# The 31-tap convolution of two recurrences: VectorE's taps behind the triangular inverse, and four taps moved from GpSimd

## The chip, the cores and the metric

The kernel runs on one core of a Trainium2 chip. The metric is the device time of one launch in microseconds (us). Engines are called PE (TensorE; PEld is its weight load), DVE (VectorE), ACT (ScalarE), POOL (GpSimd) and SP (SyncE, which issues most DMAs).

## What is computed

The reference runs two streams of 256 tokens and 1024 features, `ctx` and `x`, through two layers. Each layer normalises and modulates, projects with `w_in`, sends one half of the projection through a gated depthwise convolution of 31 taps and the other half through a linear recurrence in both directions, projects with `wo`, and ends with a SwiGLU block. The convolution, on which all of this turns:

```python
def conformer_conv(u, conv_w, conv_b, cnorm_g, cnorm_b):
    val, gate = jnp.split(u, 2, axis=-1)
    z = val * jax.nn.sigmoid(gate)
    z = dwconv(z, conv_w) + conv_b          # CONV_K = 31, 512 features
    z = group_norm(z, CONV_GROUPS, cnorm_g, cnorm_b, LN_EPS)
    return jax.nn.silu(z)
```

The recurrence is `s = s * w + sa * b + v * k` over the tokens, per head of 64, forward and backward. The kernel computes it in chunks, which needs the inverse of many small unit-triangular matrices.

## The kernel before

Activations lie feature-major, 128 features by 256 tokens; the convolution has four such blocks f0 to f3. `first()` runs the phases in this order: `wide(0, ctx)`, the first recurrence; the projections of `x`; the recurrence of layer 0 `x` beside the feed-forward of `ctx` with the middle convolution spread among them; the recurrence of layer 1 `ctx` without outputs; output and feed-forward of `x`; `wide(1, x)`, the last recurrence. A second function with no convolution of this kind runs the rest.

`wide` builds the recurrence with a filler beside it (the projection of the convolution's input, whose gated result is stored at L670 as `x0`, tile name `x` or `x0_67`, and matmuls of the modulation weights, `pb<-raw,csil`). In program order, after the whole recurrence, stands `conv`. The recurrence has these steps on the way:

- `inverse`: 31 steps, each a DVE multiply (L961) and a DVE subtract (L963), every one needing the one before.
- two DVE transposes of the result (L966, L968), small matmuls, and the building of Q: GpSimd clears its two tiles (L986), DVE and ACT copy (L982, L994) and negate (L1008, L1010).
- beside these, the products that prepare the recurrence (DVE at L1028 and L1064).
- `chain`: two groups of heads with four steps each. A step runs PE, DVE L1093, PE, ACT L1101 and DVE L1102, PE, DVE L1110 and L1111 (L1113 in a first step), and ends in the output (ACT L1130 or DVE L1132).

`conv` splits the 30 side taps of each block: the innermost to DVE as a fused multiply-add on the tile `T1c` (L725, started by L718 with the middle tap), the next to ACT (a scaled copy, L729) and the outermost to GpSimd (a scaled copy into a tile `tap`, L731). GpSimd adds every `tap`, ACT's too, into the result (L732). `tap` has two buffers, so ACT's taps and GpSimd's wait for those adds. L736 on DVE adds `T1c` to GpSimd's sum and closes a block; it needs GpSimd's last add of that block. A pair in `NPOOL` (first recurrence) or `NPOOLE` (last) gives GpSimd's and ACT's taps. With (14, 3) DVE has 13, with (12, 4) it has 14. `NPOOLC` belongs to the middle convolution (tile `z`), all of it on GpSimd.

Each engine works off its queue in order. The order is fixed ahead of time by a scheduler, which fills each engine's idle time of a simulated timeline with ready work and prefers what stands earlier in the program. So it is the schedule, and not the source, that decides that DVE's taps stand between the steps of the inverse.

Of the kernel before, what the change touches and what calls it, by code (L numbers as in the profile page):

```python
# [12 lines left out]
ALU = mybir.AluOpType  # L13
# [21 lines left out]

NLAST = 2, 4

NPOOL, NPOOLE, NPOOLC = (14, 3), (12, 4), (30, 0)
NTAP = 2

QB, QE, QC, EVERY = (2, 3, 4, 5), (2, 3, 4, 5), (1,), 2
# [217 lines left out]
class Prog:  # L259
# [427 lines left out]
    def mixed_in(self, conv, y, perm=False):  # L687

        mix = self.mixtiles()
        for f in range(NF):  # L690
            src = (conv if f < 4 else y)[:, f % 4, :]
            if perm:
                t = self.T1([P, T])
                a, b = self.unperm(t, src, True)
                self.nc.gpsimd.tensor_copy(a, b)
                src = t
            self.split(src, *mix[f])
        return mix

    def conv(self, l, z, acc, npool, hold=False):  # L700


        nc = self.nc
        o = COLS[f"convw{l}"][0]
        taps = sorted((j for j in range(31) if j != 15), key=lambda j: abs(j - 15))
        nv, na = 30 - npool[0] - npool[1], npool[1]
        parts = [("v", taps[:nv]), ("a", taps[nv : nv + na]), ("p", taps[nv + na :])]

        order = []
        for k, js in parts:  # L710
            order += [((i + 0.5) / len(js), k, j) for i, j in enumerate(js)]
        order.sort()
        zc = [acc[:, f, :] for f in range(4)]
        for f in range(4):
            w = lambda j: self.cols[:, o + 4 * j + f : o + 4 * j + f + 1]
            av = self.T1([P, T]) if nv else None
            if nv:
                nc.vector.tensor_scalar(av, z[:, f, :], w(15), None, ALU.mult)  # L718
                nc.gpsimd.memset(zc[f], 0.0)
            else:  # L720
                nc.gpsimd.tensor_scalar(zc[f], z[:, f, :], w(15), None, ALU.mult)
            for i, (_, k, j) in enumerate(order):
                d, s = slice(max(0, 15 - j), min(T, T + 15 - j)), slice(max(0, j - 15), min(T, T + j - 15))
                if k == "v":
                    nc.vector.scalar_tensor_tensor(av[:, d], z[:, f, s], w(j), av[:, d], ALU.mult, ALU.add)  # L725
                else:
                    t = self.t(self.pool, [P, T], "tap", bufs=NTAP)
                    if k == "a":
                        nc.scalar.mul(t[:, d], z[:, f, s], w(j))  # L729
                    else:  # L730
                        nc.gpsimd.tensor_scalar(t[:, d], z[:, f, s], w(j), None, ALU.mult)  # L731
                    nc.gpsimd.tensor_add(zc[f][:, d], zc[f][:, d], t[:, d])  # L732
                if i % 5 == 4:
                    yield
            if nv:
                nc.vector.scalar_tensor_tensor(zc[f], av, self.col(f"convb{l}", f), zc[f], ALU.add, ALU.add)  # L736
            else:
                nc.gpsimd.tensor_scalar(zc[f], zc[f], self.col(f"convb{l}", f), None, ALU.add)
            yield
        while hold and not self.go:  # L740
            yield
        self.group_norm(zc, f"cng{l}", f"cnb{l}", LN_EPS, AF.Silu)
# [200 lines left out]
    def inverse(self, Ld, Lo):  # L943

        nc = self.nc
        fl = lambda t: t.rearrange("p d a c x -> p (d a c) x")
        Ld, Lo = fl(Ld), fl(Lo)  # L950
        tj = self.S([P, 32, 32])
        nc.vector.transpose(tj.rearrange("p r c -> p c r"), Ld.rearrange("p j c -> p c j"))
        X = self.S([P, 32, 32])
        nc.gpsimd.memset(X, 0.0)
        xf = X.rearrange("p r c -> p (r c)")
        nc.gpsimd.memset(xf[:, 0:1024:33], 1.0)
        for k in range(31):
            m = 31 - k
            tmp = self.T1([P, 256])
            tv = tmp[:, 0 : m * (k + 1)].rearrange("p (a b) -> p a b", b=k + 1)  # L960
            nc.vector.tensor_mul(tv, tj[:, k + 1 : 32, k : k + 1].broadcast_to([P, m, k + 1]),  # L961
                                 X[:, k : k + 1, 0 : k + 1].broadcast_to([P, m, k + 1]))
            nc.vector.tensor_sub(X[:, k + 1 : 32, 0 : k + 1], X[:, k + 1 : 32, 0 : k + 1], tv)  # L963
        yield
        qt = self.S([P, 32, 32])
        nc.vector.transpose(qt, X)  # L966
        qc = self.S([P, 32, 32])
        nc.vector.transpose(qc, X.rearrange("p r c -> p c r"))  # L968

        zss = []  # L970
        for d in range(2):
            pz = self.ps((P, 16, 32))
            zs = Lo[:, 16 * d : 16 * d + 16, :]
            for j in range(16):
                J = 16 * d + j
                for h in range(2):
                    r = slice(64 * h + 32, 64 * h + 64)
                    w = slice(64 * h, 64 * h + 32)
                    self.mm(pz[w, j, :], Lo[r, J, :], qt[r, :, J], tile_position=(64 * h + 32, 64 * h))
            for h in range(2):  # L980
                w = slice(64 * h, 64 * h + 32)
                (nc.scalar.copy if h else nc.vector.tensor_copy)(zs[w], pz[w])  # L982
            zss.append(zs)
        Q = [self.S([P, 16, CH]) for _ in range(2)]
        for d in range(2):
            nc.gpsimd.memset(Q[d], 0.0)  # L986
            js = slice(16 * d, 16 * d + 16)
            src, zs = (qt, qc)[d], zss[d]
            po = self.ps((P, 16, 32))
            for q in range(4):  # L990
                s = slice(32 * q, 32 * q + 32)
                o = (q % 2) * 32
                dst, v = Q[d][s, :, o : o + 32], src[s][:, :, js].rearrange("p c j -> p j c")
                (nc.vector.tensor_copy if q % 2 else nc.scalar.copy)(dst, v)  # L994
            for j in range(16):
                J = 16 * d + j
                for h in range(2):
                    w = slice(64 * h, 64 * h + 32)
                    r = slice(64 * h + 32, 64 * h + 64)
                    if d == 0:  # L1000
                        self.mm(po[w, j, :], qc[w, :, J], zs[w, j, :], tile_position=(64 * h, 64 * h))
                    else:
                        self.mm(po[r, j, :], zs[w, j, :], qc[w, :, J], tile_position=(64 * h, 64 * h + 32))
            for h in range(2):
                w = slice(64 * h + 32 * d, 64 * h + 32 * d + 32)
                dst = Q[d][w, :, 32 * (1 - d) : 32 * (1 - d) + 32]
                if h:
                    nc.scalar.mul(dst, po[w], -1.0)  # L1008
                else:
                    nc.vector.tensor_scalar(dst, po[w], -1.0, None, ALU.mult)  # L1010
        self.Q = Q
# [626 lines left out]
```

## Time and profile before

| | us |
|---|---|
| median of 3 runs | 2772.72 (2772.6 to 2775.5) |
| the profiled execution | 2776.2 |
| its span | 2774.1 |
| PE busy | 2628.3 (95%) |
| DVE busy | 1713.4 (62%) |
| ACT busy | 1327.6 (48%) |
| POOL busy | 667.0 (24%) |

The span is what lies between the first and the last recorded instruction, 2.1 us less than the time of the execution. A busy PE is not PE at its peak, since matmul ends are modelled and its clock is granted at 1.2 or 2.4 GHz (0.50 or 1.00 of full speed). GpSimd's 667 us lie almost wholly in the stretches from 133 to 575 us (the first and the middle convolution) and from 1165 to 1280 us (the last).

### The profile page before, as it was taken

How to read it: one execution, taken by the hardware profiler on the slowest of the kernel's cores; microseconds unless marked ns; L12 is line 12 of the kernel's file. 1: busy time of each engine (PE TensorE's matmuls, PEld its weight loads, DVE VectorE, ACT ScalarE, POOL GpSimd, SP SyncE). 2: the span in 40 equal slices, each digit the busy share in tenths (PEclk: the TensorE clock that was granted, in tenths of full speed). 3: DMA queues.
4: the chain of work that ended last, by engine and by line, in shares of the span. 5: the costliest groups of instructions: out<-in, count | busy, mean ns of one | idle time of the engine just before them, and what ended most of it. 6: DMA issues, size and time to landing. Idle time of an engine off the chain costs nothing.

```text
span 2774.1 us, 53770 instructions
## 1 busy us (share of the span) xinstructions
PE 2628.3 (95%) x22398; PEld 2288.3 (82%) x22398; DVE 1713.4 (62%) x2703; ACT 1327.6 (48%) x2015; POOL 667.0 (24%) x669
## 2 busy tenths in 40 slices
PE   7889988999889998899899899999999999999998
PEld 4866867888678897866799899889899898889897
DVE  3885778655577555984555655666655655755655
ACT  5533654434564346433544544654544544644543
POOL 0287999920130001384200000010000000100000
PEclk9989989999999999979899999999999999999999
DMA  7244424434323354234355555524555554525653
GB/s 251 102 153 167 153 86 167 139 129 145 137 77 115 130 181 148 100 138 153 124 188 183 198 184 188 188 86 157 183 186 186 183 186 172 170 85 183 205 185 119
DMA packets 118767, 430.70 MB, mean 155 GB/s; under 512 B 13174, under 2 KB 13686, under 8 KB 118524
## 3 DMA queue, kind: packets, MB, share of 16 engines
q1 hardware_dynamic: 118524, 427.28, 44.7%
q8 instruction: 175, 2.87, 0.4%
q14 instruction: 68, 0.56, 0.1%
HBM read 425.13 MB, written 2.10 MB: 154 GB/s over the span
## 4 chain that ended last, share of the span: by engine, by line
PE 76%; DVE 10%; POOL 5%; ACT 5%; issue 2%; DMA 2%; SPq 0%; ACTq 0%; POOLq 0%; DVEq 0%
PE pb L333 32%; PE acc L333 24%; PE ps L333 19%; POOL tap L731 3%; DVE wl L342 2%; POOL z L732 1%; DVE T1c L725 1%; DMA raw<-in_ada 1%; DVE S L963 1%; DVE T L961 1%; POOL x L732 1%; ACT wh L341 1%; PE acc L438 0%; DMA raw<-in_wr 0%; ACT L384 0%
## 5 line engine op out<-in xcount | busy, mean ns | idle before, releaser
L342 DVE TENSOR_TENSOR wl<-raw,wh 128x1024 fp32r<-128x1024 f32 (+1 forms) x654 | 814.5, 1249 | 621.6 <-ACT wh L341 390.9
L341 ACT CAST wh<-raw 128x1024 fp32r<-128x1024 f32 (+1 forms) x654 | 681.8, 1046 | 892.7 <-PE pb L333 349.8
L333 PE MATMUL pb<-xf,wh 128*128 128x256 f32 (+1 forms) x2560 | 488.1, 289 | 15.6 <-DVE T1b L588 5.2
L333 PE MATMUL pb<-S,wh 128*128 128x256 f32 x2560 | 490.9, 289 | 4.3 <-DVE S L462 1.8
L333 PEld LDWEIGHTS pb<-xf,wh 128*128 128x128 f32 (+1 forms) x2560 | 411.3, 195 | 29.7 <-DVE T1b L588 8.8
L333 PEld LDWEIGHTS pb<-S,wh 128*128 128x128 f32 x2560 | 407.7, 192 | 21.5 <-issue 11.7
L333 PE MATMUL ps<-S,wh 128*128 128x256 f32 x2048 | 390.6, 288 | 0.5 <-ACT S L460 0.4
L333 PE MATMUL pb<-xf,wl 128*128 128x256 f32 (+1 forms) x1280 | 372.8, 292 | 8.9 <-DVE wl L342 8.9
L365 POOL TENSOR_TENSOR wl<-raw,wh 128x1024 fp32r<-128x1024 f32 x22 | 52.1, 2379 | 1340.7 <-ACT wh L364 824.2
L333 PE MATMUL pb<-S,wl 128*128 128x256 f32 x1280 | 367.4, 287 | 2.1 <-DVE wl L342 2.1
L333 PEld LDWEIGHTS ps<-S,wh 128*128 128x128 f32 x2048 | 327.0, 192 | 9.4 <-issue 3.7
L333 PE MATMUL ps<-S,wl 128*128 128x256 f32 x1024 | 293.8, 287 | 0.6 <-DVE wl L342 0.6
L333 PEld LDWEIGHTS pb<-xf,wl 128*128 128x128 f32 (+1 forms) x1280 | 249.3, 195 | 16.9 <-DVE wl L342 11.7
L333 PEld LDWEIGHTS pb<-S,wl 128*128 128x128 f32 x1280 | 245.3, 192 | 7.0 <-issue 3.2
L333 PE MATMUL acc<-wh,T 128*128 128x512 f32 x704 | 206.3, 393 | 0.0
L333 PEld LDWEIGHTS ps<-S,wl 128*128 128x128 f32 x1024 | 196.7, 192 | 3.0 <-issue 1.5
L333 PE MATMUL acc<-wh,T1b 128*128 128x512 f32 x528 | 158.6, 399 | 3.5 <-ACT T1b L341 3.5
L731 POOL TENSOR_SCALAR tap<-z,cols 128x255 f32<-128x255 f32 (+14 forms) x120 | 154.4, 1295 | 0.0
L333 PEld LDWEIGHTS acc<-wh,T 128*128 128x128 f32 x704 | 127.0, 189 | 23.6
L731 POOL TENSOR_SCALAR tap<-x,cols 128x246 f32<-128x246 f32 (+6 forms) x104 | 112.9, 1093 | 46.1 <-DVE x L670 46.0
L333 PEld LDWEIGHTS acc<-wh,T1b 128*128 128x128 f32 x528 | 94.9, 190 | 22.3 <-ACT T1b L341 4.4
L333 PE MATMUL acc<-wl,T 128*128 128x512 f32 x352 | 113.3, 395 | 0.0
(445 smaller groups left out, 3956.7 us busy)
## 6 DMA issues: line engine op xcount, KB each, us to landing
raw<-in_fu SPq DMA_DIRECT2D x132, 512.0 KB, 3.2
raw<-in_ada SPq DMA_DIRECT2D x96, 512.0 KB, 4.2
raw<-in_pu SPq DMA_DIRECT2D x88, 512.0 KB, 4.3
raw<-in_qu SPq DMA_DIRECT2D x88, 512.0 KB, 4.2
raw<-in_fd SPq DMA_DIRECT2D x66, 512.0 KB, 3.2
raw<-in_wr SPq DMA_DIRECT2D x51, 512.0 KB, 3.9
raw<-in_pd SPq DMA_DIRECT2D x44, 512.0 KB, 4.3
raw<-in_qd SPq DMA_DIRECT2D x44, 512.0 KB, 4.3
```

What stands on the lines that cost most here:

```text
L333: return self.nc.tensor.matmul(out, lhsT, rhs, start=start, stop=stop, **kw)
L341: self.nc.scalar.copy(hi, src)
L342: self.nc.vector.tensor_sub(lo, src, hi.bitcast(F32))
L365: self.nc.gpsimd.tensor_sub(lo, r, hi.bitcast(F32))
L725: nc.vector.scalar_tensor_tensor(av[:, d], z[:, f, s], w(j), av[:, d], ALU.mult, ALU.add)
L731: nc.gpsimd.tensor_scalar(t[:, d], z[:, f, s], w(j), None, ALU.mult)
L732: nc.gpsimd.tensor_add(zc[f][:, d], zc[f][:, d], t[:, d])
L961: nc.vector.tensor_mul(tv, tj[:, k + 1 : 32, k : k + 1].broadcast_to([P, m, k + 1]), X[:, k : k + 1, 0 : k + 1].broadcast_to([P, m, k + 1]))
L963: nc.vector.tensor_sub(X[:, k + 1 : 32, 0 : k + 1], X[:, k + 1 : 32, 0 : k + 1], tv)
```

## The change

Two things change. The pairs of taps become (10, 3) and (9, 3): in the first recurrence DVE takes four taps more of each block and GpSimd four fewer; in the last DVE takes four more, GpSimd three fewer and ACT one fewer. And the first DVE instruction of each block is not issued before the last subtract of the inverse.

```diff
-NPOOL, NPOOLE, NPOOLC = (14, 3), (12, 4), (30, 0)
+NPOOL, NPOOLE, NPOOLC = (10, 3), (9, 3), (30, 0)
...
             if nv:
-                nc.vector.tensor_scalar(av, z[:, f, :], w(15), None, ALU.mult)
+                with self.tc.issue_after(self.inverted.ins):
+                    nc.vector.tensor_scalar(av, z[:, f, :], w(15), None, ALU.mult)
                 nc.gpsimd.memset(zc[f], 0.0)
...
-            nc.vector.tensor_sub(X[:, k + 1 : 32, 0 : k + 1], X[:, k + 1 : 32, 0 : k + 1], tv)
+            self.inverted = nc.vector.tensor_sub(X[:, k + 1 : 32, 0 : k + 1], X[:, k + 1 : 32, 0 : k + 1], tv)
```

Behind L718 all line numbers grow by one. The change moves instructions in the queues, so here is what stands there at three places.

DVE's queue in the first recurrence, near the end of the inverse, before:

```order
L725 SCALAR_TENSOR_TENSOR T1c_3011<-x_67,cols,T1c_3011 128x252
L961 TENSOR_TENSOR T_205_1273<-S_1187,S_1189 128x112
L725 SCALAR_TENSOR_TENSOR T1c_3011<-x_67,cols,T1c_3011 128x252
L963 TENSOR_TENSOR S_1189<-S_1189,T_205_1273 128x4x28
L725 SCALAR_TENSOR_TENSOR T1c_3011<-x_67,cols,T1c_3011 128x251
L961 TENSOR_TENSOR T_206_1276<-S_1187,S_1189 128x87
L725 SCALAR_TENSOR_TENSOR T1c_3011<-x_67,cols,T1c_3011 128x251
L963 TENSOR_TENSOR S_1189<-S_1189,T_206_1276 128x3x29
```

The same place with the change:

```order
L962 TENSOR_TENSOR T_207_1279<-S_1187,S_1189 128x60
L964 TENSOR_TENSOR S_1189<-S_1189,T_207_1279 128x2x30
L962 TENSOR_TENSOR T_208_1282<-S_1187,S_1189 128x31
L964 TENSOR_TENSOR S_1189<-S_1189,T_208_1282 128x31
L719 TENSOR_SCALAR T1c_2875<-x_67,cols 128x256
L719 TENSOR_SCALAR T1c_2935<-x_67,cols 128x256
L726 SCALAR_TENSOR_TENSOR T1c_2875<-x_67,cols,T1c_2875 128x255
L726 SCALAR_TENSOR_TENSOR T1c_2935<-x_67,cols,T1c_2935 128x255
```

The taps leave the inverse and start right behind its last subtract, two blocks side by side; the transpose L967 (before L966) comes 16 rows later.

DVE's queue in the first recurrence, around the step that closes the fourth block (L736, then L737, on `x1_68`), before, from the last L1102 of the chain on:

```order
L1102 TENSOR_SCALAR xf_261_1607<-acc10_424_2673 64x2x128
L342 TENSOR_TENSOR wl_578_3279<-raw_576_3276,wh_577_3278 128x1024
L1110 TENSOR_TENSOR st_426_2693<-acc11_425_2684,st_412_2585 128x256
L1111 TENSOR_TENSOR st_426_2693<-st_426_2693,pc_149_884 128x256
...
L342 TENSOR_TENSOR wl_586_3343<-raw_584_3340,wh_585_3342 128x1024
L736 SCALAR_TENSOR_TENSOR x1_68<-T1c_531_3079,cols_69,x1_68 128x256
L936 TENSOR_TENSOR T1_467_2835<-acc00_466_2831,S_62_299 128x256
```

With the change:

```order
L1094 TENSOR_TENSOR T1_359_2299<-acc00_358_2290,Sb_243_1503 128x256
L1065 TENSOR_TENSOR T2_274_1677<-acc11_272_1667,const_70 64x256
L1065 TENSOR_TENSOR T2_274_1677<-acc10_273_1668,const_70 64x256
L1103 TENSOR_SCALAR xf_242_1502<-acc00_361_2302 64x2x2x64
L1065 TENSOR_TENSOR T2_277_1690<-acc11_275_1680,const_70 64x256
L503 TENSOR_TENSOR mod0_82<-pb_378_2388,cols_69 128x8
L508 SCALAR_TENSOR_TENSOR mod0_82<-mod0_82,cols_69 128x16
L737 SCALAR_TENSOR_TENSOR x1_68<-T1c_519_3055,cols_69,x1_68 128x256
L1065 TENSOR_TENSOR T2_277_1690<-acc10_276_1681,const_70 64x256
L1103 TENSOR_SCALAR xf_261_1607<-acc10_333_2183 64x2x2x64
```

Before, the closing step stands behind the whole chain. Now it stands behind two of the chain's eight L1103 steps and ahead of the other six.

DVE's queue in the last recurrence, around the same closing step, before:

```order
L1111 TENSOR_TENSOR st_2388_14152<-st_2388_14152,pc_2170_12672 128x256
L1102 TENSOR_SCALAR xf_2282_13395<-acc10_2414_14262 64x2x2x64
L1093 TENSOR_TENSOR T1_2426_14338<-acc00_2425_14329,Sb_2264_13291 128x256
L736 SCALAR_TENSOR_TENSOR x1_68<-T1c_2527_14821,cols_69,x1_68 128x256
L503 TENSOR_TENSOR mod1_83<-pb_2410_14244,cols_69 128x8
L1110 TENSOR_TENSOR st_2416_14282<-acc11_2415_14273,st_2360_14023 128x256
```

With the change:

```order
L1065 TENSOR_TENSOR T2_2282_13446<-acc10_2281_13437,const_70 64x256
L737 SCALAR_TENSOR_TENSOR x1_68<-T1c_2499_14765,cols_69,x1_68 128x256
L1094 TENSOR_TENSOR T1_2340_13968<-acc10_2339_13959,Sb_2267_13364 128x256
L1094 TENSOR_TENSOR T1_2368_14097<-acc00_2367_14088,Sb_2248_13259 128x256
L1103 TENSOR_SCALAR xf_2266_13363<-acc10_2342_13971 64x2x2x64
L1103 TENSOR_SCALAR xf_2247_13258<-acc00_2370_14100 64x2x2x64
```

Before, four of the eight L1102 steps stand ahead of it; now one, and seven follow.

## Rows read from the trace of the kernel before

**Rows 1.** The chain of waits of the page: its share by engine.
```profile
PE 76%; DVE 10%; POOL 5%; ACT 5%; issue 2%; DMA 2%; SPq 0%; ACTq 0%; POOLq 0%; DVEq 0%
```

**Rows 2.** Busy time by stretch: us, engines with instructions, PE clock, DMA share, GB/s.
```profile
1170.00:1180.00 10.00, 8.05 (x112) 7.23 (x112) 10.00 (x18) 2.11 (x4) 9.68 (x11) 1.00 0.30 107
380.00:440.00 60.00, 44.71 (x606) 36.82 (x605) 49.53 (x69) 33.69 (x65) 59.63 (x59) 0.86 0.23 80
```

**Rows 3.** Busy time by stretch of DVE alone, first and last recurrence's inverse.
```profile
113.00:187.50 74.50, 68.14 (x155) 0.89 0.44 149
1149.00:1220.00 71.00, 69.65 (x155) 0.95 0.45 157
```

**Rows 4.** The same stretches, T1c's instructions alone: PE, PEld, DVE, ACT, then clock.
```profile
113.00:187.50 74.50, 0.00 (x0) 0.00 (x0) 26.10 (x43) 0.00 (x0) 0.89 0.44 149
1149.00:1220.00 71.00, 0.00 (x0) 0.00 (x0) 26.52 (x46) 0.00 (x0) 0.95 0.45 157
```

**Rows 5.** DVE's timeline, first recurrence: start us, duration us, line, operation, [idle before].
```profile
187.18 0.17 DVE L963 TENSOR_TENSOR S<-S,T 128x31 f32<-128x31 f32 x1
187.38 1.25 DVE L966 STREAM_TRANSPOSE S<-S 128x1024 f32<-128x1024 f32 x1
188.55 1.92 DVE L968 STREAM_TRANSPOSE S<-S 128x1024 f32<-128x1024 f32 x1
190.39 0.38 DVE L1064 TENSOR_TENSOR T<-acc,const 64x256 f32<-64x256 f32 x1
190.80 3.47 DVE L994 COPY S<-S 32x512 f32<-32x512 f32 x4
...
224.65 0.43 DVE L1102 TENSOR_SCALAR xf<-acc 64x256 f32<-64x256 f32 x1 [2.04 <-PE acc L333]
...
264.59 0.43 DVE L1102 TENSOR_SCALAR xf<-acc 64x256 f32<-64x256 f32 x1 [0.58 <-PE acc L333]
...
277.49 0.69 DVE L736 SCALAR_TENSOR_TENSOR x<-T1c,cols,x 128x256 f32<-128x256 f32 x1
```

**Rows 6.** One line's instructions: count, shortest, median and longest ns, first and last start.
```profile
L725 DVE SCALAR_TENSOR_TENSOR T1c<-x,cols,T1c x108: 459/568/1021, 134.6 to 1243.9; 128x255 f32<-128x255 f32 x16, 128x254 f32<-128x254 f32 x16, 128x253 f32<-128x253 f32 x16, 128x252 f32<-128x252 f32 x16
L732 POOL TENSOR_TENSOR x<-x,tap x132: 691/716/1618, 134.9 to 1279.2; 128x247 f32<-128x247 f32 x16, 128x246 f32<-128x246 f32 x16, 128x245 f32<-128x245 f32 x16, 128x244 f32<-128x244 f32 x16
L731 POOL TENSOR_SCALAR tap<-x,cols x104: 888/1038/2128, 133.0 to 1277.5; 128x246 f32<-128x246 f32 x16, 128x245 f32<-128x245 f32 x16, 128x244 f32<-128x244 f32 x16, 128x243 f32<-128x243 f32 x16
```

**Rows 7.** GpSimd's timeline, first recurrence: start us, duration us, line, [idle before].
```profile
133.03 1.89 POOL L731 TENSOR_SCALAR tap<-x,cols 128x247 f32<-128x247 f32 x2 [24.08 <-DVE x L670]
...
276.46 2.81 POOL L731 TENSOR_SCALAR tap<-z,cols 128x255 f32<-128x255 f32 x2
```

**Rows 8.** What GpSimd's adds (L732) of both convolutions waited for: us, times.
```profile
  ACT tap L729: 28.5, 8
```

**Rows 9.** DVE's timeline, last recurrence, same columns as rows 5.
```profile
1219.48 0.39 DVE L963 TENSOR_TENSOR S<-S,T 128x31 f32<-128x31 f32 x1
...
1279.91 0.48 DVE L736 SCALAR_TENSOR_TENSOR x<-T1c,cols,x 128x256 f32<-128x256 f32 x1 [5.61 <-POOL x L732]
...
1295.83 0.43 DVE L1102 TENSOR_SCALAR xf<-acc 64x256 f32<-64x256 f32 x1
```

**Rows 10.** ACT's timeline, last recurrence, same columns: a tap, then chain steps.
```profile
1274.29 0.50 ACT L729 ACTIVATE tap<-x,cols 128x247 f32<-128x247 f32 x1 [4.93 <-POOL x L732]
...
1288.45 0.38 ACT L1101 ACTIVATE xf<-acc 64x256 f32<-64x256 f32 x1
1292.00 0.38 ACT L1101 ACTIVATE xf<-acc 64x256 f32<-64x256 f32 x1 [3.17 <-PE acc L333]
```

**Rows 11.** GpSimd's timeline, last recurrence: the first tap.
```profile
1165.26 1.00 POOL L731 TENSOR_SCALAR tap<-x,cols 128x246 f32<-128x246 f32 x1 [21.90 <-DVE x L670]
```

**Rows 12.** Chain of waits, 380 to 440 us (start, us, what), and one wait there.
```profile
395.68 5.09 POOL S L847 x2
...
DVE T L961 <- POOL S L956: 4.9, 1, 4.9
```

## The prediction

> **What bounds the kernel now.** I read the chain of waits first: PE holds 76% of it, DVE 10%, POOL 5% [rows 1]. Outside the two long recurrences the weights' matmuls fill PE, and there a change to DVE or GpSimd is worth nothing. So the question is only what PE loses in three stretches: the first recurrence (113 to 270 us), the last (1149 to 1300 us), and 380 to 440 us, where GpSimd works at the middle convolution. I read busy time by stretch next. In 1170 to 1180 us PE is busy 8.05 of 10 us while DVE shows 10.00 and POOL 9.68 [rows 2]: the inverse and the taps share a full DVE, and the splits of weights that feed PE stand in the same queue. In 380 to 440 us PE misses 15.3 of 60 us, POOL is busy 59.63 [rows 2], and POOL stands on the chain of waits there: two L847 take 5.09 us, and an inverse waits 4.9 us for a GpSimd memset [rows 12]. Last come the timelines of DVE, ACT and GpSimd, for what ends when.
>
> **Term 1: the inverse loses its taps.** From its start to its last subtract DVE is busy 68.14 of 74.5 us in the first recurrence and 69.65 of 71 us in the last [rows 3]. Of this the taps are 26.10 us (43 instructions, 0.607 each) and 26.52 us (46, 0.577 each) [rows 4]. All of them go behind the inverse. Its last subtract ends at 187.4 and 1219.9 us now [rows 5, 9]; without the taps it would end at 161.3 and 1193.4 us. I add about 2 us of waits for PE that the taps filled until now: 163 and 1195 us.
>
> **Term 2: what DVE must do behind it.** The taps come back, and more of them. In the first recurrence a block has 17 + L718 + L736, which is 19 for each of four blocks and 76 in all (60 before); in the last 18 + 2, so 80 (64 before). At 0.607 and 0.577 us that is 46.1 and 46.2 us. By the order with the change these stand, with some 40 others, ahead of L737 of the fourth block, and ahead of most of the chain. The others are 15 or 16 of L1064 at about 0.4 us (6.3 us), the two transposes (3.2), four L994 (3.5) [rows 5], and some 20 smaller ones, for which I estimate 6.6 us from instructions of this size: 19.6 us. So DVE reaches the closing step at 163 + 46.1 + 19.6 = 228.7 us in the first recurrence, and at 1195 + 46.2 + 19.6 = 1260.8 us in the last. In the first recurrence two chain steps are done by then, in the last one.
>
> **Term 3: GpSimd.** A tap takes 1.04 us and an add 0.72 (medians) [rows 6]. The first recurrence loses 16 of each, 28.2 us; the last 12 taps and 16 adds, 24.0 us (four of these adds were for ACT's taps, which cost ACT 0.50 us each [rows 10] and are otherwise free). GpSimd's first convolution runs from 133.0 to 276.5 us [rows 7]. It would end at 248 if its waits for ACT's taps stay, and at 220 if all 28.5 us of these [rows 8] go. ACT's taps now stand in ACT's queue behind copies that wait for the transposes, so some stay: I take 238 us. The last runs from 1165.3 to 1279.9 us [rows 9, 11] and would end near 1256, ahead of DVE.
>
> **Term 4: a new wait.** Before, L736 of the fourth block stood behind the chain's eight L1102 and ran at 277.5 us, after the last of them at 264.6 [rows 5]; nothing stood behind it that mattered. Now L737 needs GpSimd's last add with six chain steps queued behind it. In the first recurrence DVE is there at 228.7 and GpSimd at 238: DVE stands for 9 us, and the chain with it, PE's outputs of the recurrence next. In the last recurrence GpSimd comes first and the wait costs nothing; it costs what GpSimd is late beyond 1260.8 if ACT's taps come late.
>
> **Term 5: the chain's end.** A step without taps between takes 3.6 us (L1101 at 1288.45 and 1292.00) [rows 10]. Before, ACT's taps, each waiting for a GpSimd add (4.93 us at 1274.29 [rows 10]), stood between the steps; with the change the last of ACT's taps comes before the second step. First: 238 + 6 x 3.6 = 259.6 against 264.6 us [rows 5], a gain of 5.0. PE has filler in either case, and the same amount of it. Last: 1260.8 + 7 x 3.6 = 1286.0 against 1295.8 [rows 9], a gain of 9.8.
>
> **Term 6: the middle convolution.** GpSimd turns to it about 38 us earlier (238 against 276.5), and the same number of its instructions, 111, stands between its start and the first L365 in both orders. So at 380 us GpSimd should no longer be late. It can give back at most the 15.3 us that PE misses there [rows 2] and at least nothing, since L847 and the memset still run there. I take 7 us, near the middle and close to the 5.09 and 4.9 us of rows 12 together with little else.
>
> **Sum.** 5.0 + 9.8 + 7 = 21.8 us off the profiled execution's 2776.2 us: 2754.4. That execution lies 3.5 us above the median 2772.72, so the forecast is 2751 us. Ends: the first term runs from a loss of 5 (GpSimd at 248) to a gain of 14 (DVE decides at 228.7); the last from a gain of 19 (taps at the shortest 0.459 us [rows 6]) to a loss, below; the middle from 0 to 15.
>
> **A rule against it.** A tap takes 0.459 us at its shortest, 0.568 in the median and 1.021 at its longest [rows 6], and the mean beside a GpSimd that was busy 9.68 of 10 us was 0.577. The Trainium skill says in "SBUF — State Buffer", section "SBUF: two separate sides", that VectorE with two SBUF inputs and GpSimd take a shared port pair as an exclusive lock, and the loser blocks for the other's whole instruction. By that every tap that meets a GpSimd instruction would pay for it in full, which is the first rival below with a price beyond it. The trace agrees only in part: both engines show nearly 10 of 10 us busy at once, and the taps are stretched by a quarter, not doubled; but recorded times can hold waiting.
>
> **Rivals.** (a) Taps that stand in a row next to GpSimd are stretched more than those between the inverse's steps. At 0.92 us, near the longest, the first recurrence has DVE at the closing step at 163 + 69.9 + 19.6 = 252.5 and the chain's end at 274.1, 9.5 us late; the last has 1195 + 73.6 + 19.6 + 25.2 = 1313.4, 17.6 late. With nothing from the middle the kernel takes 2772.7 + 27 = 2800 us. It decides from 0.79 us a tap in the first recurrence and 0.70 in the last. Against it: the means of rows 4 were taken beside the same GpSimd instructions. (b) The closing step's wait and PE's fill eat the first recurrence: GpSimd at 248, no gain in the middle because the recurrence there is later reached by the same in-order queue, and only the last recurrence's 9.8 less 5 stays: 2768 us, within 0.2%. (c) All three stretches pay in full, 14 + 19 + 15: 2725 us. For it speaks that PE also lost clock there; against it that DVE's queue is full in each case. (d) The change doesn't do what it says: taps still between the inverse's steps. The order excludes it.
>
> **How the numbers follow.** A run of this kernel can tell about 0.2% from no change, 5.5 us: faster is below 2767.2, slower above 2778.3. Forecast (gain of 8 to 36 us): 0.64. (c): 0.07. (b), from 2764 to 2778: 0.16, a fifth of it faster. (a): 0.13, nearly all slower. So faster 0.74, same 0.13, slower 0.13. The range 2733 to 2777 holds the forecast's own spread and (b), and leaves out most of (a) and (c).
>
> **What would show it.** Right: the last subtract near 163 and 1195 us; the fourth L737 near 238 (after a wait for GpSimd) and 1261; the last L1103 near 260 and 1286; T1c at 0.55 to 0.62 us behind the inverse; GpSimd's middle convolution from 238 us and PE missing about 8 us in 380 to 440. Wrong: a T1c mean above 0.7, the closing step waiting beyond 248, an inverse that still ends after 175 or 1205 because PE and not DVE paced it, or PE missing as much as before around 380 to 440.

## The result: slower by 1.2%

The change takes 2806.4 us (median of four runs) against 2772.7 us before, a ratio of 1.0119 (95% interval 1.0103 to 1.0135). Forecast were 2751 us. I split each profiled execution at four events of DVE's timeline: the start of the first inverse (first L961), the last L1102 of the first chain, the start of the last inverse, the last L1102 of the last chain (starts, each time). A stage's time is that of one profiled execution of its kernel.

| us | before | change | difference |
|---|---|---|---|
| first inverse's start to first chain's end | 151.2 | 163.8 | +12.6 |
| first chain's end to last inverse's start | 885.1 | 882.2 | -2.9 |
| last inverse's start to last chain's end | 146.1 | 167.0 | +20.9 |
| the whole span | 2774.1 | 2803.7 | +29.6 |

The loss lies in the two recurrences. DVE's timeline of the change (start us, duration us, line, operation, [idle before]; all lines behind L718 are one higher than before), first and last recurrence, answers to [rows 5, 9]:

```profile
111.92 0.19 DVE L962 TENSOR_TENSOR T<-S,S 128x31 f32<-128x31 f32 x1
...
161.18 0.57 DVE L964 TENSOR_TENSOR S<-S,T 128x31 f32<-128x31 f32 x1
...
193.34 0.68 DVE L1011 TENSOR_SCALAR S<-ps 32x512 f32<-32x512 f32 x1
214.14 0.43 DVE L1103 TENSOR_SCALAR xf<-acc 64x256 f32<-64x256 f32 x1
...
230.59 0.43 DVE L1103 TENSOR_SCALAR xf<-acc 64x256 f32<-64x256 f32 x1
...
235.77 0.48 DVE L737 SCALAR_TENSOR_TENSOR x<-T1c,cols,x 128x256 f32<-128x256 f32 x1 [3.12 <-POOL x L733]
...
275.74 0.43 DVE L1103 TENSOR_SCALAR xf<-acc 64x256 f32<-64x256 f32 x1
```

```profile
1157.93 0.20 DVE L962 TENSOR_TENSOR T<-S,S 128x31 f32<-128x31 f32 x1
...
1201.62 0.60 DVE L964 TENSOR_TENSOR S<-S,T 128x31 f32<-128x31 f32 x1
...
1254.81 0.43 DVE L1103 TENSOR_SCALAR xf<-acc 64x256 f32<-64x256 f32 x1
...
1274.39 0.47 DVE L737 SCALAR_TENSOR_TENSOR x<-T1c,cols,x 128x256 f32<-128x256 f32 x1
...
1324.94 0.43 DVE L1103 TENSOR_SCALAR xf<-acc 64x256 f32<-64x256 f32 x1
```

Before, each inverse begins and the first of the chain's L1102 runs at:

```profile
113.44 0.19 DVE L961 TENSOR_TENSOR T<-S,S 128x31 f32<-128x31 f32 x1
...
218.06 0.43 DVE L1102 TENSOR_SCALAR xf<-acc 64x256 f32<-64x256 f32 x1
```

```profile
1149.68 0.22 DVE L961 TENSOR_TENSOR T<-S,S 128x31 f32<-128x31 f32 x1
...
1255.92 0.43 DVE L1102 TENSOR_SCALAR xf<-acc 64x256 f32<-64x256 f32 x1 [4.49 <-PE acc L333]
```

The inverse ends about where it was forecast, 24 and 26 us sooner after its start than before (at 161.8 us, and 44.3 us after its start in the last recurrence). The closing step L737 comes at 235.8 and 1274.4 us. But the chain, which had its eight L1102 in 46.5 us in the first and 39.9 in the last recurrence before (first L1102 to last), now takes 61.6 and 70.1 us. It begins sooner and ends later.

**What stands behind the taps.** The products of L1064 (now L1065) prepare the chain's two groups and stand in DVE's queue among the taps. Their rows before and after, first and then last recurrence (count: shortest/median/longest ns, first to last start):

```profile
L1064 DVE TENSOR_TENSOR T<-acc,const x16: 376/416/418, 174.4 to 217.6; 64x256 f32<-64x256 f32 x16
L1064 DVE TENSOR_TENSOR T<-acc,const x16: 402/408/418, 1206.0 to 1242.1; 64x256 f32<-64x256 f32 x16
```

```profile
L1065 DVE TENSOR_TENSOR T<-acc,const x16: 405/412/417, 173.4 to 236.2; 64x256 f32<-64x256 f32 x16
L1065 DVE TENSOR_TENSOR T<-acc,const x16: 404/408/417, 1214.6 to 1274.1; 64x256 f32<-64x256 f32 x16
```

The last product comes 19 us later in the first recurrence and 32 us later in the last (20 and 24 later counted from the inverse's start). Before, all sixteen were done when the chain's first L1102 ran; now seven and six of them fall between the chain's steps. The matmuls behind a product wait in PE's queue, and whatever stands behind them there waits too.

**What happened to the filler.** SyncE's loads of modulation weights show it for the last recurrence: each row is a run of loads, with the time from its first to its last and their count. Before:

```profile
1191.62 67.63 SPq L348 DMA_DIRECT2D raw<-in_ada  x21
...
1263.41 9.91 SPq L348 DMA_DIRECT2D raw<-in_ada  x7
```

With the change:

```profile
1200.58 23.47 SPq L348 DMA_DIRECT2D raw<-in_ada  x7
...
1267.48 11.86 SPq L348 DMA_DIRECT2D raw<-in_ada  x6
...
1282.55 19.73 SPq L348 DMA_DIRECT2D raw<-in_ada  x14
```

Each view begins in the middle: 4 loads had gone out before it in the kernel before and 5 with the change, of 32 in all. Before, 25 loads were out by 1259 us and 7 fell into the rest of the chain. Now 12 are out by 1224 us, none goes out between 1224 and 1267 us, and 20 follow at the chain's steps.

The matmuls that these loads feed (`csil`), counted in the chain from its first L1102 to its last, are in the first recurrence before and with the change, then in the last before and with the change (us, PE busy with count, PE clock, DMA share, GB/s):

```profile
218.10:264.60 46.50, 13.25 (x58) 0.99 0.62 216
214.10:275.70 61.60, 13.11 (x48) 0.81 0.39 138
1255.90:1295.80 39.90, 10.20 (x48) 0.94 0.69 249
1254.80:1324.90 70.10, 23.55 (x96) 0.78 0.57 204
```

So the last chain carries twice the filler of before, and the first, which also grew, carries less.

Two rows of the last recurrence's chain of waits with the change (start us, us, what), 9.2 us together, and the busy time in the middle of its taps (us; PE, PEld, DVE, ACT, POOL with instructions; PE clock, DMA share, GB/s):

```profile
1294.77 4.78 DMA raw<-in_ada
...
1306.93 4.38 DMA raw<-in_wo
```

```profile
1240.00:1250.00 10.00, 5.88 (x66) 4.75 (x65) 9.90 (x17) 2.53 (x5) 9.60 (x12) 0.50 0.04 15
1250.00:1260.00 10.00, 8.91 (x76) 6.73 (x77) 9.90 (x22) 1.38 (x3) 7.94 (x9) 0.50 0.01 2
```

In these 20 us DVE is full with taps, PE idles for 5 us and works at half its clock, and the DMA engines nearly stand still. Before, the stretch of Q had the half clock and the still DMA too, but PE was busy throughout:

```profile
1230.00:1240.00 10.00, 10.00 (x163) 8.57 (x160) 7.68 (x16) 3.11 (x6) 8.24 (x10) 0.50 0.01 2
```

The half clock also lasts longer now. With the change it begins just after the taps (PE busy for 1.41 of 5 us, then the clock at 0.50). Two rows of PE there, then PE from the start of the last inverse to the last chain step, before and with the change:

```profile
1200.00:1205.00 5.00, 1.41 (x10) 0.91 0.60 219
1205.00:1210.00 5.00, 4.59 (x20) 0.50 0.27 101
```

```profile
1149.70:1295.80 146.10, 134.03 (x1813) 0.86 0.45 160
1157.90:1324.90 167.00, 146.81 (x1820) 0.76 0.39 140
```

**GpSimd beside alternating taps.** In the first recurrence there is a second thing. GpSimd's row of one run of taps, DVE's, and then ACT and PE:

```profile
L732 POOL TENSOR_SCALAR tap<-x,cols x40: 892/986/9775, 131.4 to 233.4; 128x245 f32<-128x245 f32 x8, 128x244 f32<-128x244 f32 x8, 128x243 f32<-128x243 f32 x8, 128x242 f32<-128x242 f32 x8
```

```profile
198.82 10.83 POOL L732 TENSOR_SCALAR tap<-x,cols 128x243 f32<-128x243 f32 x2
199.38 2.82 DVE L726 SCALAR_TENSOR_TENSOR T1c<-x,cols,T1c 128x253 f32<-128x253 f32 x7
202.20 6.69 DVE L726 SCALAR_TENSOR_TENSOR T1c<-x,cols,T1c 128x252 f32<-128x252 f32 x17
211.12 0.50 ACT L730 ACTIVATE tap<-x,cols 128x246 f32<-128x246 f32 x1 [13.16 <-POOL x L733]
211.53 0.56 ACT L1071 COPY Sb<-acc 128x512 f32<-128x512 f32 x1
212.15 0.80 PE L333 MATMUL acc<-S,S 64*64 64x64 f32 x5 [6.30 <-ACT Sb L1071]
```

One GpSimd tap takes 9.8 us (0.99 in the median) while DVE runs 23 taps with nothing but one small addition (L503) between, 17 of them in 6.69 us. GpSimd's add is late by that, ACT's tap waits 13.16 us for a buffer, the copy L1071 stands behind it, and PE waits 6.30 us for the copy.

### The profile page after: what moved, and what is told of

The parts are those of the page before. It is cut to its first block, busy times and chain, and to the rows that moved or that the text cites. A ratio compares the mean times of both kernels' runs of the same rounds, so it can differ in the third digit from the quotient of the medians.

```text
span 2803.7 us, 53741 instructions
## 1 busy us (share of the span) xinstructions
PE 2638.3 (94%) x22398; PEld 2294.1 (82%) x22398; DVE 1729.0 (62%) x2735; ACT 1325.0 (47%) x2012; POOL 620.3 (22%) x609
## 4 chain that ended last, share of the span: by engine, by line
PE 77%; DVE 13%; ACT 4%; issue 2%; POOL 2%; DMA 2%; SPq 0%; DVEq 0%; ACTq 0%; POOLq 0%
PE pb L333 32%; PE acc L333 24%; PE ps L333 19%; DVE wl L342 3%; DVE T1c L726 1%; DVE T L962 1%; DVE S L964 1%; POOL tap L732 1%; ACT wh L341 1%; DMA raw<-in_ada 1%; DVE acc L619 1%; POOL x L733 0%; PE acc L438 0%; DVE x L620 0%; DVE tDb L519 0%
## 5 line engine op out<-in xcount | busy, mean ns | idle before, releaser
L333 PE MATMUL pb<-xf,wh 128*128 128x256 f32 (+1 forms) x2560 | 485.1, 287 | 10.6 <-DVE S L630 3.5
L732 POOL TENSOR_SCALAR tap<-z,cols 128x255 f32<-128x255 f32 (+14 forms) x120 | 151.4, 1270 | 0.0
L733 POOL TENSOR_TENSOR z<-z,tap 128x255 f32<-128x255 f32 (+14 forms) x120 | 109.5, 912 | 3.8
```

Source lines behind the costliest of these rows:

```text
L333: return self.nc.tensor.matmul(out, lhsT, rhs, start=start, stop=stop, **kw)
```

## The experiments

The times from the start of the inverse to the first L1102 of the chain on DVE's timeline and to the last, and PE's mean granted clock between the inverse's start and that last step, of every run; the ratio is that of the whole kernel to the kernel before.

| kernel | first: to chain, to its end, clock | last: to chain, to its end, clock | ratio (95%) |
|---|---|---|---|
| before | 104.6, 151.2, 0.86 | 106.2, 146.1, 0.86 | |
| change | 102.2, 163.8, 0.83 | 96.9, 167.0, 0.76 | 1.0119 (1.0103 to 1.0135) |
| e1 tie alone | 94.7, 157.7, 0.82 | 89.3, 148.4, 0.85 | 1.0058 (1.0037 to 1.0079) |
| e2 counts alone | 113.4, 148.6, 0.87 | 118.2, 151.7, 0.85 | 1.0008 (0.9992 to 1.0024) |
| e3 first alone | 103.0, 165.4, 0.79 | 109.3, 155.4, 0.82 | 1.0074 (1.0047 to 1.0100) |
| e4 last alone | 104.3, 150.8, 0.86 | 98.8, 152.2, 0.83 | 1.0023 (1.0011 to 1.0036) |
| e6 change, no loads | 104.0, 164.7, 0.79 | 92.6, 146.4, 0.87 | 1.0049 (1.0033 to 1.0064) |
| e7 before, no loads | 104.6, 151.0, 0.86 | 111.7, 144.6, 0.82 | 0.9991 (0.9980 to 1.0003) |
| e8 blocks in turn | 97.3, 160.4, 0.81 | 92.9, 153.7, 0.83 | 1.0040 (1.0026 to 1.0055) |
| e9 behind Q | 90.0, 168.1, 0.79 | 91.3, 165.5, 0.76 | 1.0156 (1.0134 to 1.0178) |
| e11 behind products | 91.5, 153.2, 0.87 | 83.1, 156.1, 0.84 | 1.0039 (1.0025 to 1.0053) |
| e12 the same, old counts | 83.8, 152.8, 0.87 | 89.7, 165.1, 0.81 | 1.0064 (1.0042 to 1.0085) |
| e13 first count alone, no tie | 116.3, 152.2, 0.84 | 104.1, 157.8, 0.83 | 1.0035 (1.0022 to 1.0049) |

Three things limit what a row can say. Executions of one kernel differ by several us: those of the kernel before took 2771.5 to 2785.0 us beside e1 to e4, and the profiled ones of e2 and e13 lie 10 and 8 us above their kernels' medians. Kernels with the same source in the first recurrence end it within 1.6 us of each other (150.8 to 151.2 in before, e4 and e7; 163.8 to 165.4 in the change, e3 and e6). And every edit has the whole schedule made anew: e13, which ties nothing and moves four taps of each block in one recurrence, costs 0.35%, so a difference of this size is no proof of a mechanism by itself.

### Which half of the change: e1 and e2

```diff
-NPOOL, NPOOLE, NPOOLC = (10, 3), (9, 3), (30, 0)     # e1: the change with the counts of before
+NPOOL, NPOOLE, NPOOLC = (14, 3), (12, 4), (30, 0)
```

> DVE's taps tied behind the inverse, counts as before: (14, 3) and (12, 4). Theory 1 (the tie is the cause: the taps in one block delay DVE's products L1029 and L1065, so PE's queue with the modulation weights' matmuls stands, and these fall into the chain): slower than before by 15 to 30 us, 2788 to 2803 us. Rival (the counts are the cause: 16 taps more on DVE in each recurrence): within 5 us of before, 2768 to 2778.

e2 is the kernel before with the new counts.

> The new counts (10, 3) and (9, 3), DVE's taps free to stand between the inverse's steps. Theory 1: no loss, since GpSimd ends some 25 us earlier in each recurrence and ACT's taps leave the chain: 2755 to 2775 us. Rival (counts): DVE, full during the inverse, ends it 16 x 0.6 = 10 us later in each recurrence, 2785 to 2795 us.

The tie alone costs 0.58%, the counts alone nothing that can be told from no change. Theory 1 held, the rivals fell (e2's 2777.4 us lie 2.4 above theory 1's range, with the kernel before at 2776.7 beside it). In e2 DVE does end the inverse some 9 us later in the first and 15 in the last recurrence (83.3 and 85.7 us against 73.9 and 70.2), as the rival says, but the chain then takes 35 and 34 us in place of 46.5 and 39.9. That is the first sign that reaching the chain sooner or later is worth little by itself. Together the two halves cost twice the tie alone; that with more taps there is more to stand behind is how I read it, and no run isolates it.

### Which recurrence: e3 and e4

```diff
-                with self.tc.issue_after(self.inverted.ins):                                      # e3; the last keeps (12, 4)
+                with self.tc.issue_after(self.inverted.ins) if l == 0 else contextlib.nullcontext():
```

> Tie and new counts in the first recurrence alone. From the trace of the change, where the last chain step of the first recurrence comes 11.1 us later (275.7 against 264.6) and 2.8 us come back before the last: 2781 us (2777 to 2785). If the two recurrences act on each other through the schedule, it lies outside of that.

e4 is its counterpart: `l == 1`, and the first recurrence keeps (14, 3).

> Tie and new counts in the last recurrence alone. From the trace of the change, where the last recurrence takes 20.8 us longer than before: 2794 us (2789 to 2799). With the first alone this adds up to the change if the two are independent.

Both expectations missed. Each changed recurrence behaves as an altered one (165.4 and 152.2), but the first alone costs 0.74%, since the last recurrence, whose source is that of before, takes 155.4 in place of 146.1 us; and the last alone costs 6 us in place of 20.9. The two act on each other. The likely way is the schedule, which is made anew for the whole program with each edit, so that the filler and its loads come to lie elsewhere.

### Do the loads pace the last chain: e6 and e7

```diff
-                        r = self.raw(f"ada{l}", nb * 4 + k4 * 2 + k2)
+                        r = self.const if l == 1 and tuple(qs) == QE else self.raw(f"ada{l}", nb * 4 + k4 * 2 + k2)
```

> The change, with the modulation weights of the last recurrence's filler not loaded: its 128 matmuls read a constant that lies in SBUF, so it leaves out 32 loads of 512 KB (and the outputs are not the reference's). Theory 2 (in the change the filler falls into the last chain and is paced there by its loads, DMA share 0.82): the chain's last step comes 10 to 20 us sooner after the start of the last inverse than the 167.0 us of the change, and this kernel is within 10 us of the next one outside the first recurrence. Rival (DVE's taps and the half clock pace the chain): the chain still ends 160 us or more after the start of the inverse.

> The kernel before with the same loads left out; the other half of the pair. Before, the chain's last step comes 146.1 us after the start of the last inverse with a DMA share of 0.64 to 0.74 in the chain: theory 2 expects 140 to 146 us here, so that the change's loss of 20.8 us in this stretch shrinks to under 10 us between the two.

Without these loads the change's last recurrence takes 146.4 us and that of before 144.6: of 20.9 us of loss 1.8 are left. The kernel before gains 1.5 us there, the change 20.6. Busy time of the last chain of the change, with its loads and without (columns as above), then the filler's matmuls without the loads, and PE from the inverse's start to the last step:

```profile
1254.80:1324.90 70.10, 65.81 (x814) 41.54 (x812) 30.28 (x70) 14.38 (x27) 14.66 (x18) 0.78 0.57 204
```

```profile
1261.80:1315.60 53.80, 46.46 (x737) 33.46 (x738) 28.54 (x67) 10.32 (x23) 19.72 (x24) 0.84 0.04 12
1261.80:1315.60 53.80, 10.56 (x44) 0.84 0.04 12
1169.20:1315.60 146.40, 128.98 (x1822) 0.87 0.14 45
```

So the last recurrence's loss hangs on the filler and its loads, as theory 2 said. That the loads set the pace there is not shown, because three things changed at once without them: the waits for them went (9.2 us of the chain of waits above), 44 of the filler's matmuls are left in the chain in place of 96, and PE's mean clock over the recurrence is 0.87 in place of 0.76. The last is as large as the gain: by my estimate, time x (1 - clock), the clock withheld 39 us of 167.0 with the loads and 19 of 146.4 without. The rival of this run, taps and half clock, fell only for the taps; the half clock went with the loads.

Nor does the early start pay without the loads: e6 reaches the chain 19 us sooner than e7 and ends it 1.8 us later. In the first recurrence, whose filler is untouched here, the change stays at 164.7 us.

### Is it GpSimd's long tap: e8

```diff
-                with self.tc.issue_after(self.inverted.ins):
+                with self.tc.issue_after((last if f else self.inverted).ins):
...
-                    nc.vector.scalar_tensor_tensor(av[:, d], z[:, f, s], w(j), av[:, d], ALU.mult, ALU.add)
+                    last = nc.vector.scalar_tensor_tensor(av[:, d], z[:, f, s], w(j), av[:, d], ALU.mult, ALU.add)
```

> The change, but each block's first DVE tap issued after the last DVE tap of the block before, so the taps of two blocks no longer alternate. Theory 3 (alternating taps leave no gap, and GpSimd gets nothing done beside them: one GpSimd tap of 9.8 us beside a run of 17 DVE taps of 0.39 us each; its add, ACT's tap and PE wait for it): GpSimd's longest tap falls to 2.2 us or less, DVE's taps rise to 0.50 us or more, and the first recurrence's chain ends 4 to 9 us sooner than the 163.8 us after the inverse's start; 2795 to 2803 us in all. Rival (the long tap costs nothing): the chain's end unchanged within 2 us.

GpSimd's and DVE's taps in the first recurrence of e8:

```profile
L732 POOL TENSOR_SCALAR tap<-x,cols x40: 887/1066/1986, 129.3 to 226.7; 128x245 f32<-128x245 f32 x8, 128x244 f32<-128x244 f32 x8, 128x243 f32<-128x243 f32 x8, 128x242 f32<-128x242 f32 x8
L726 DVE SCALAR_TENSOR_TENSOR T1c<-x,cols,T1c x68: 428/563/873, 159.9 to 224.1; 128x255 f32<-128x255 f32 x8, 128x254 f32<-128x254 f32 x8, 128x253 f32<-128x253 f32 x8, 128x252 f32<-128x252 f32 x8
```

The mechanism is as expected: with one block at a time GpSimd's longest tap is 1.99 us, and DVE's taps take 0.563 us in the median (0.468 in the change). Its price was set a little too high: the first recurrence gains 3.4 us, under the 4 to 9 expected. The whole came out better than expected, at 1.0040, because the last recurrence gained 13.3 us, for which this run gives no cause of its own. Its last chain has as many of the filler's matmuls as the change (96, and 20 loads), so their number alone doesn't set its length; the clock there is 0.91 in place of 0.78:

```profile
1247.70:1308.50 60.80, 23.33 (x96) 0.91 0.65 220
```

### What the taps must not stand ahead of: e9, e11, e12

e9 ties the taps behind the last DVE step of Q (counts of before), e11 and e12 behind the last of the sixteen products (the diff is e11's):

```diff
-            self.inverted = nc.vector.tensor_sub(X[:, k + 1 : 32, 0 : k + 1], X[:, k + 1 : 32, 0 : k + 1], tv)
+            nc.vector.tensor_sub(X[:, k + 1 : 32, 0 : k + 1], X[:, k + 1 : 32, 0 : k + 1], tv)
...
-                    nc.vector.tensor_mul(ga[:, h], pg[h],          # L1065, in the products
+                    self.inverted = nc.vector.tensor_mul(ga[:, h], pg[h],
```

> Counts as before, the taps tied behind the last DVE step of building Q (L1010 of before) in place of the inverse. Theory 1 (what costs is what stands behind the taps between the inverse and Q: the products, the transposes, Q's copies): Q some 15 us earlier than with the tie behind the inverse, 2765 to 2785 us. Rival (any tie costs, because the taps then meet the chain): as the tie alone, 2790 us or more.

e9 is the worst of all, as its rival said and beyond it. With no tap ahead of Q, its last step L1011 still comes at 193.8 us, against 193.3 in the change, and waits for PE:

```profile
193.78 0.68 DVE L1011 TENSOR_SCALAR S<-ps 32x512 f32<-32x512 f32 x1 [4.61 <-PE ps L333]
```

Counted from the inverse's start Q is 2 us sooner than in e1, which has the same counts (79.9 and 81.9 us), and 1 us sooner in the last recurrence, not 15. So Q hardly waited for the taps, and my reading of theory 1 was wrong in that. What makes e9 worse than e1 isn't shown. Its last product comes at 227.6 and 1284.5 us, counted from the inverse's start no later than in e1 in the first recurrence (113.7 and 113.4) and 7 us later in the last. 24 us lie between the first chain step and the second (203.9 and 228.2), and in them one GpSimd addition takes 7.73 us.

> The new counts, the taps tied behind the last DVE product (L1064 of before, the second group's) in place of the inverse. In the change that product comes at 236.2 and 1274.1 us, before at 217.6 and 1242.1. Theory 1 (the taps hold up the products, and with them PE's queue and the filler behind it): the last product comes 10 us or more sooner than in the change, the second chain step less than 10 us after the first (16.5 in the change, 6.6 before), the two recurrences 5 us or more shorter each; 2775 to 2797 us. Rival (DVE's work behind the inverse is what counts, wherever it stands): within 5 us of the change, 2801 to 2811.

```profile
L1065 DVE TENSOR_TENSOR T<-acc,const x16: 404/416/417, 171.8 to 213.9; 64x256 f32<-64x256 f32 x16
L1065 DVE TENSOR_TENSOR T<-acc,const x16: 404/416/418, 1204.4 to 1242.0; 64x256 f32<-64x256 f32 x16
```

With the products ahead of the taps the last of them comes at 213.9 and 1242.0 us, and both recurrences are shorter than in the change, by 10.6 and 10.9 us. The whole is 1.0039, in the range of theory 1 and outside the rival's. The gain lies ahead of the chain: from its first step to its last it takes 61.7 and 73.0 us, no less than in the change. The gap to the second chain step missed its mark (11.3 and 22.7 us); the taps, which now stand in the chain, are the likely reason.

> As the run behind the products, with the counts of before. Theory 1: 3 to 12 us under the tie alone (1.0058 of before), so 2765 to 2790 us; if the chain stays short with the taps in its gaps it is faster than before. Rival: taps in the chain's queue cost as much as taps ahead of it, 2790 us or more.

At 1.0064 the rival of this run held: it reaches the chain 21 and 17 us sooner than before and ends it 1.6 and 19 us later. The chain, not the way to it, grows. Against e1, with the same counts, the last recurrence has its last product 9 us sooner after the inverse's start and yet ends 16.7 us later, so there late products are not what decides.

### A version that beats both: e13

> The kernel before with the new count in the first recurrence alone, nothing tied. In the run with both new counts untied, the first recurrence took 148.6 us to its last chain step (151.2 before) and the last 151.7 (146.1). If that carries over: 2 to 3 us gained in the first and none lost in the last, 2765 to 2775 us. If the middle gives it back: 2775 to 2785.

It doesn't: 1.0035. The first recurrence is 1.0 us longer, not 2 to 3 shorter, and the last, unchanged in its source, takes 157.8 us, in an execution 8 us above its kernel's median. No version that I ran beats the kernel before.

## Why the prediction was wrong

**Term 1 held.** The inverse ends at 161.8 us (163 forecast) and 44.3 us after its start in the last recurrence (45.3).

**Term 2 held by its sum and not by its parts.** The closing step was reached within 6 us of the forecast, counted from the inverse's start. But all of T1c's instructions took 37.1 and 44.6 us (0.488 and 0.557 each), less than the 46.1 and 46.2 forecast:

```profile
161.70:236.50 74.80, 0.00 (x0) 0.00 (x0) 37.09 (x76) 0.00 (x0) 0.75 0.43 149
1202.20:1275.00 72.80, 0.00 (x0) 0.00 (x0) 44.59 (x80) 0.00 (x0) 0.56 0.23 85
```

What they saved DVE lost in waits: it stood idle for 20.5 and 11.7 us between the inverse's end and the closing step, mostly for PE (15.1 and 11.3). Rival (a), which has the nearest time (2800 us), is wrong in its mechanism: the taps were not stretched, GpSimd was.

**Terms 3 and 4 held.** GpSimd was forecast to end at 238 us; L737 ran at 235.8, after a wait of 3.1 us (9 forecast). One bound of term 3 was misread: the 28.5 us of [rows 8] are waits of both convolutions, 20.0 of them in the first, so the early end was 228 us and not 220. The 238 taken lies within either.

**Term 6 was mis-sized.** PE's idle time in 380 to 440 us fell from 15.3 [rows 2] to 11.0 us, and the middle took 2.9 us less; 7 were forecast.

```profile
380.00:440.00 60.00, 49.04 (x521) 40.69 (x520) 48.90 (x67) 34.89 (x65) 58.40 (x57) 0.86 0.22 79
```

**Term 5 failed.** It priced a chain step at 3.6 us, from two steps near the end of the last chain [rows 10], and said that PE has the same filler in either case. Behind the closing step the six steps of the first recurrence took 40.0 us and the seven of the last 50.6, that is 6.7 and 7.2 us each, against 21.6 and 25.2 forecast. These 44 us are most of the 55 us between forecast and result; the late closing step of the last recurrence and term 6 add 5 and 4. The row priced only the last steps. Before, too, a step of the first chain took 6.6 us on average and one of the last 5.7 (46.5 and 39.9 us over seven), and in the last chain the loads of modulation weights had all gone out by 1273 us, ahead of the two steps priced.

What made the steps long differs between the recurrences. In the last the filler was not the same: 96 of its matmuls stood in the chain in place of 48, and without their loads the loss falls from 20.9 to 1.8 us (e6, e7). In the first the filler in the chain was fewer (48 for 58), and what grew is the rest: seven products of the chain's own preparation came between its steps, PE's idle time in it rose from 1.6 to 6.1 us, and its clock fell from 0.99 to 0.81. With the taps behind the products (e11) 10.6 of the 12.6 us come back, and the clock with them (0.87 over the recurrence, 0.86 before). GpSimd's long tap is part of this and not a sum on top: e8 alone gives back 3.4, and e11 has no long tap in the first recurrence either.

None of the signs of being wrong that the prediction lists came. What missed was a sign of being right: the last L1103, forecast near 260 and 1286 us, came at 275.7 and 1324.9.

**What stays open.** Why the last recurrence grows by 9 to 12 us when only the first is edited (e3, e13) was not isolated. It goes with the schedule that is made anew, but no run held the order of the last recurrence fixed. The half clock is a rival that no run separates from the waits. By the estimate above it withheld 20.5 us of each recurrence before, and 27 and 39 us with the change: 7 and 19 us more, beside losses of 12.6 and 20.9. In the table, too, the long recurrences are with few exceptions those with a low clock. With the change it fell when PE ran short of work, so it may be the way in which the waiting costs, or a cost beside it. Why e9 is worse than e1, and e12 in its last recurrence too, stays open as well.

## What to carry to other kernels

Time to the start of a serial stage can be worth nothing by itself if an in-order engine must also do filler: count what filler, which loads and which of the stage's own operands are left when it begins, before and after, and price the stage with them. Take the price of a step from the whole stage and not from its last steps. When work is tied behind a step, list everything that now stands behind that work on its own engine, and above all the small operands that another engine's queue waits for. A wait made for a critical chain can be right on its own terms, as it was here for the inverse, and still lose more at the next engine.

## What the runs showed of the hardware

GpSimd can be held up almost wholly by VectorE: one tap of 0.99 us in the median took 9.8 us beside 23 VectorE multiply-adds with two SBUF inputs, 17 of them in 6.69 us. The Trainium skill's rule ("SBUF — State Buffer", section "SBUF: two separate sides"), that the two take a port pair as an exclusive lock and the loser blocks, agrees with this row in that GpSimd blocked; I had weighed it as a risk for VectorE, and the loser was GpSimd, over a run of instructions and not one. The same came back in the first recurrence of e6 (9.26 us) and the last of e11 and e12 (8.02 and 6.98), and a GpSimd addition took 7.73 us in e9. Each time the taps of two blocks alternated on VectorE, but alternating alone doesn't do it: in the last recurrence of the change and of e4, and in e1, where they alternate too, the longest tap is 2.1 us. With one block at a time (e8) none was longer than 2.13, and none in the kernel before, whose taps stand between the inverse's steps.
